# The fourth block of the recurrent gates: one plain matmul replaced by three on rounded parts, with a gather by DMA

## The chip, the cores and the metric

The kernel runs on 1 core of one Trainium2 chip. The metric is the device time of one execution in microseconds, the median of the runs shown; lower is better. TensorE is PE in the profile, VectorE DVE, ScalarE ACT, GpSimd POOL, and SP is the queue that issues most DMAs.

## The reference, cut to what matters

One inference step of two layers on 1056 tokens (1024 of a prompt, 32 of eight decoding sequences). Layer 0 is a recurrent block, layer 1 a gated linear attention. What the change touches is the pair of gates of layer 0, block diagonal with 16 blocks of 96 channels:

```python
xh = xf.reshape(Bsz, T, N_BLK, BLK_W)
r = jax.nn.sigmoid(jnp.einsum('btni,nij->btnj', xh, w_r.astype(jnp.float32)).reshape(Bsz, T, W) + b_r)
ig = jax.nn.sigmoid(jnp.einsum('btni,nij->btnj', xh, w_i.astype(jnp.float32)).reshape(Bsz, T, W) + b_i)
log_a = -LRU_C * jax.nn.softplus(-lam.astype(jnp.float32)) * r
a = jnp.exp(log_a)
bterm = jnp.sqrt(-jnp.expm1(2.0 * log_a)) * (ig * xf)
```

`xf` is the output of a causal convolution of width 4; `a` and `bterm` go into a scan over the tokens.

## The kernel before, in words

Activations stand with channels in the 128 partitions and tokens in the columns, in three chunks of 352. Products of layer 0 are exact to nearly float32 by splitting: each operand x becomes a rounded high part (an ACT copy to `F32R`) and a low part (x minus the high part, on DVE or POOL), and `mm3` (L244 to L248) makes three matmuls, high by high, high weight by low, low weight by high. A plain `F32` matmul is used in a few places, among them the one that the change replaces.

The 1536 recurrent channels are permuted into four groups of three tiles of 128. In a group, tile j holds its own block of 96 channels and, at partitions 32j to 32j+31, a third of the group's fourth block. The gates of the three own blocks are `mm3` on the tiles' parts `X` with weights `gh` and `gl` (L571), where rows and columns of the fourth block are zero. For the fourth block the three pieces of 32 partitions have to come together in one tile of 96:

- `conv` (L472): when a chunk of a tile's convolution output `t` is done, a DMA of 32 partitions puts the piece into `ST` (L512), which has all three chunks; then ACT and DVE make the parts in `X` (L514, L515).
- `lru` (L547): per chunk and per gate, a plain matmul of `ST` with the fourth block's weights `gs` (L577), a tanh into `td` (L579), and three DMAs that put its pieces back into the gate tiles `R` (L583). Two gates, three chunks, four groups: 24 such matmuls. `gs` is loaded once a group (L557).

Program order and engine order differ. Every operation is recorded in a `Flow` (L52) with an engine, an estimated length, what it reads and writes, and a priority. `Flow.run` (L188) tries several list schedules with these lengths and a random search of the opening, and emits the best in its order; so on every engine the operations of many stages are interleaved, and a changed length or dependence reorders all of layer 0. Layer 1 has a `Flow` of its own. 48 filler matmuls on constants (L739) stand at lowest priority in the opening. Products take turns in four PSUM banks `mm`, gates and norms in four banks `hg`. Weights of 128x512 go through a ring of three raw buffers `wraw` and are split into `whi` and `wlo`. In the opening, the squares of the input are summed (ACT L440 into `xo`, DVE L443) for the norm, while the first six products already run on inputs that are not yet normalized; L537 is the first evacuation of such a product by DVE.

Of the kernel before, what the change touches and what calls it, by code (L numbers as in the profile page):

```python
# [14 lines left out]
F32 = mybir.dt.float32  # L15
F32R = mybir.dt.float32r
# [22 lines left out]
NB = 8  # L39
# [175 lines left out]
def tile_trunk(ctx: ExitStack, tc: tile.TileContext, xT, prm, hc, w0, wg, wo0, w1, wo1, s_in,  # L215
# [85 lines left out]
    with ExitStack() as l0:  # L301
# [49 lines left out]
        xbs = ring("xb", 3, 384)  # L351
# [120 lines left out]
        def conv(g, head=False):  # L472

            items = []
            for j in range(3):
# [3 lines left out]
                def evac(c, ps, pk, by=None, j=j, m=m, mine=mine):  # L479
# [18 lines left out]
                    if c == 2:  # L498
                        xs = xb[:, 323:379].rearrange("p (b j) -> p b j", j=7)
                        pool(24, lambda: G.tensor_copy(xs[:, :, :3], cs[:, m]), (("hct",),), (xk,), 1)  # L500
                        act(32, lambda: S.copy(xs[:, :, 3:], ps[:, n:CH].rearrange("p (b j) -> p b j", j=4)), (pk,), (xk,), 0)
                        pool(3, lambda: G.tensor_copy(cst[:, m, 0, :], xb[:, 320:323]), (xk,), (("cst", m),), 4)
                        pool(24, lambda: G.tensor_copy(cst[:, m, 1:, :], xs[:, :, 4:7]), (xk,), (("cst", m, 1),), 4)
                        parts.append((xs, t[:, n:].rearrange("p (b j) -> p b j", j=4), lambda ap, i: ap[:, :, i:i + 4], 32))
# [6 lines left out]
                    w = slice(32 * j, 32 * j + 32)  # L511
                    dma(ST[w, chunk(c)], t[w], (tk,), (("ST", j, c),), 1, 45)  # L512
# [34 lines left out]
        def lru(g):  # L547
# [9 lines left out]
            dma(gs.rearrange("p a b -> p (a b)"), wg[g][:96, 768:], (), (("gs",),), 2, 74)  # L557
            prev = [(0.0, None)] * 3
            for c in range(NCH):
# [4 lines left out]
                tak, tik = ([("R", s, i, j) for j in range(3)] for i in range(2))  # L564
                for i, hb in ((0, hbr), (1, hbi)):
                    for j in range(3):
# [9 lines left out]

                    fl.add("PE", 0.62, lambda ps=ps, i=i, c=c: T.matmul(ps[:96, :CH], gs[:, i, :], ST[:96, chunk(c)], start=True, stop=True),  # L577
                           (("gs",), *(("ST", j, c) for j in range(3))), (pk,), 0)
                    act(CH, lambda ps=ps, i=i: S.activation(td[:, i], ps[:96, :CH], AF.Tanh, bias=hbd[:96, 4 * i + g:4 * i + g + 1],  # L579
                                                            scale=0.5), (pk, ("sm",)), (("td", i),), 2, 0.05)  # L580
                    for j in range(3):
                        w = slice(32 * j, 32 * j + 32)
                        dma(R[w, i, j], td[w, i], (("td", i),), (("R", s, i, j),), 2, 45)  # L583
# [16 lines left out]
                for j in range(3):  # L600
                    m = 3 * g + j
                    aj, bj = ab[:, j], ti[:, j]
                    if c == 2:
                        a0 = aj[:, 320:].rearrange("p (b j) -> p b j", j=4)[:, :, 0]
                        b0 = bj[:, 320:].rearrange("p (b j) -> p b j", j=4)[:, :, 0]
                        dve(8, lambda a0=a0, j=j, m=m: V.tensor_tensor(t0[:, j], a0, h0[:, m], op=ALU.mult),
                            (("a", s, j), ("hct",)), (("t0", j),), 3)
                        dve(8, lambda b0=b0, j=j: V.tensor_tensor(b0, b0, t0[:, j], op=ALU.add), (("t0", j), tik[j]), (tik[j],), 3)
                        dve(8, lambda a0=a0: V.memset(a0, 0.0), (), (("a", s, j),), 3)
# [130 lines left out]
        g0 = fixed("g0", [128, 8])  # L740
# [1197 lines left out]
```

## Time and profile before

| | |
|---|---|
| median of 3 runs | 1071.77 us (1071.49 to 1074.11) |
| the profiled execution's own time | 1068.75 us |
| its span (first to last instruction) | 1067.0 us |
| granted TensorE clock, mean | 0.993 |
| PE, DVE, ACT, POOL busy | 98%, 73%, 63%, 47% of the span |
| L577 matmuls | 24, recorded as 48 of 458 ns |

How to read it: a line is named by the number in the kernel and a group by output and inputs (`hg<-ST,gs`). A matmul's recorded length overlaps the next one's, so what a matmul costs is read from the distance between starts. An idle stretch of an engine that the end does not wait for costs nothing.

### The profile page before, as it was taken

The numbers are of one execution on the slowest core, as the hardware profiler recorded it, in microseconds if no ns is written. First come the engines' busy times: TensorE is split into PE (matmuls) and PEld (weight loads), VectorE is DVE, ScalarE is ACT, GpSimd is POOL, SyncE is SP. The second block draws the span as 40 slices with busy tenths as digits, with TensorE's granted clock in tenths as the row PEclk, the third lists the DMA queues.
The fourth block names the chain that finished last, engine by engine and source line by source line (L and its number), as shares of the span: only waits on it lengthen the run. The fifth ranks groups of instructions, "written<-read, shape, count | busy, mean of one in ns | idle before, by whom it ended". The sixth has DMA issues, their size and how long they took to land.

```text
span 1067.0 us, 25951 instructions
## 1 busy us (share of the span) xinstructions
PE 1046.7 (98%) x10120; PEld 1019.2 (96%) x10120; DVE 782.0 (73%) x1533; ACT 676.2 (63%) x1526; POOL 505.5 (47%) x528
## 2 busy tenths in 40 slices
PE   9999999999999999999989999999999989999997
PEld 9999999999999999999979999999999989999996
DVE  7999996888888688265786666656566576898636
ACT  6568656867765874243468685858586755865443
POOL 3425443454443456455544445455554454335354
PEclk9999999999999999999999999999999999999998
DMA  9111112124842685363685475756476652734634
GB/s 302 60 27 45 55 49 74 57 61 114 248 142 59 201 278 158 119 216 123 197 217 110 114 169 103 173 111 167 98 180 130 169 123 83 254 95 112 142 72 163
DMA packets 90331, 143.24 MB, mean 134 GB/s; under 512 B 11104, under 2 KB 55904, under 8 KB 90208
## 3 DMA queue, kind: packets, MB, share of 16 engines
q1 hardware_dynamic: 74656, 112.46, 33.2%
q0 software_dynamic: 13248, 26.35, 14.9%
q10 hardware_dynamic: 2304, 2.77, 0.8%
q8 instruction: 79, 1.29, 0.5%
q14 instruction: 44, 0.36, 0.1%
HBM read 81.60 MB, written 33.05 MB: 107 GB/s over the span
## 4 chain that ended last, share of the span: by engine, by line
PE 88%; DVE 7%; DMA 2%; ACT 1%; issue 1%; POOL 0%; POOLq 0%; ACTq 0%; SPq 0%; DVEq 0%
PE mm L246 24%; PE mm L248 24%; PE mm L247 24%; PE hg L1061 2%; PE hg L1278 1%; PE hg L577 1%; PE hg L1170 1%; PE hg L1280 1%; PE hg L1224 1%; PE hg L246 1%; PE hg L247 1%; PE hg L248 1%; DVE sg L1043 1%; DMA wlo<-wraw 1%; PE hg L1322 1%
## 5 line engine op out<-in xcount | busy, mean ns | idle before, releaser
L246 PE MATMUL mm<-xh,whi 128*128 128x352 f32 (+1 forms) x1147 | 354.7, 309 | 4.1 <-ACT os L1248 2.6
L247 PE MATMUL mm<-xl,whi 128*128 128x352 f32 (+1 forms) x1147 | 348.5, 304 | 0.0
L248 PE MATMUL mm<-xh,wlo 128*128 128x352 f32 (+1 forms) x1147 | 348.3, 304 | 0.0
L246 PEld LDWEIGHTS mm<-xh,whi 128*128 128x128 f32 x1147 | 215.5, 188 | 7.5 <-ACT os L1248 2.8
L247 PEld LDWEIGHTS mm<-xl,whi 128*128 128x128 f32 x1147 | 215.7, 188 | 1.7 <-issue 0.2
L248 PEld LDWEIGHTS mm<-xh,wlo 128*128 128x128 f32 x1147 | 215.6, 188 | 0.0
L333 POOL TENSOR_TENSOR wlo<-wraw,whi 128x512 fp32r<-128x512 f32 (+1 forms) x66 | 94.3, 1437 | 92.7 <-ACT whi L388 75.7
L248 PE MATMUL mm<-t,wlo 128*128 128x264 f32 x408 | 116.6, 286 | 3.8 <-DMA wlo<-wraw 3.8
L246 PE MATMUL mm<-t,whi 128*128 128x264 f32 x408 | 118.9, 291 | 0.0
L247 PE MATMUL mm<-t,whi 128*128 128x264 f32 x408 | 116.5, 286 | 0.0
L509 DVE SCALAR_TENSOR_TENSOR k<-xb,prm_sb,k 128x352 f32<-128x352 f32 (+2 forms) x144 | 90.1, 637 | 10.9 <-ACT k L506 6.1
L248 PEld LDWEIGHTS mm<-t,wlo 128*128 128x128 f32 x408 | 77.4, 190 | 4.2 <-DMA wlo<-wraw 4.2
L246 PEld LDWEIGHTS mm<-t,whi 128*128 128x128 f32 x408 | 77.6, 190 | 0.3
L247 PEld LDWEIGHTS mm<-t,whi 128*128 128x128 f32 x408 | 77.7, 190 | 0.1
L1540 DVE TENSOR_TENSOR k<-mm,k 128x264 f32<-128x264 f32 x72 | 30.6, 430 | 52.5 <-PE mm L248 50.4
L320 POOL DMA_DIRECT2D wlo<-wraw x51 | 44.5, 885 | 51.5 <-ACT wlo L319 35.6
L592 POOL TENSOR_TENSOR k<-X 128x352 f32<-128x352 f32 x36 | 43.8, 1226 | 47.6 <-DVE R L593 37.9
L246 PE MATMUL mm<-yh,whi 128*128 128x352 f32 x153 | 49.9, 326 | 0.0
L248 PE MATMUL mm<-yh,wlo 128*128 128x352 f32 x153 | 49.4, 323 | 0.0
L247 PE MATMUL mm<-yl,whi 128*128 128x352 f32 x153 | 49.4, 323 | 0.0
L388 ACT CAST whi<-wraw 128x512 fp32r<-128x512 f32 (+1 forms) x63 | 36.3, 591 | 20.2 <-DMA wraw<-in_w_dram 10.0
L320 POOL DMA_DIRECT2D wlo<-R x30 | 28.1, 936 | 43.1 <-ACT wlo L319 40.6
(425 smaller groups left out, 2724.2 us busy)
## 6 DMA issues: line engine op xcount, KB each, us to landing
wraw<-in_w_dram SPq DMA_DIRECT2D x88, 256.0 KB, 3.5
wlo<-wraw POOLq DMA_DIRECT2D x51, 256.0 KB, 4.0
wlo<-R POOLq DMA_DIRECT2D x30, 256.0 KB, 4.2
wraw<-in_wo_dram SPq DMA_DIRECT2D x37, 192.0 KB, 3.0
ysum<-sg SPq DMA_DIRECT2D x9, 528.0 KB, 4.0
si<-in_s_in_dram SPq DMA_DIRECT2D x8, 512.0 KB, 4.5
R<-in_w_dram SPq DMA_DIRECT2D x16, 256.0 KB, 3.3
out_ss_out_dram<-si SPq DMA_DIRECT2D x8, 512.0 KB, 2.7
```

The costliest lines, as they stand in the source:

```text
L246: T.matmul(out, wh, xh, start=first, stop=False, skip_group_check=chained)
L247: T.matmul(out, wh, xl, start=False, stop=False, skip_group_check=chained)
L248: T.matmul(out, wl, xh, start=False, stop=last, skip_group_check=chained)
L320: fl.add("POOL", 0.93, lambda: G.dma_start(dst.bitcast(F32), src, accum_op=ALU.add), (*r, *w), w, prio, n / 2)
L333: emit = lambda: e.tensor_tensor(b, x, a.bitcast(F32), op=ALU.subtract)
L388: act(m, lambda hi=hi, raw=raw, m=m: S.copy(hi[:, :m], raw[:, :m]), rk, (hk,), prio)
L509: dve(u, lambda src=src, dst=dst, sh=sh, k=k: V.scalar_tensor_tensor(dst, sh(src, k), pc("cw", 12 * k + m), dst, op0=ALU.mult, op1=ALU.add ...
L577: fl.add("PE", 0.62, lambda ps=ps, i=i, c=c: T.matmul(ps[:96, :CH], gs[:, i, :], ST[:96, chunk(c)], start=True, stop=True), (("gs",), *((" ...
L592: pool(CH, lambda x=x, a=a, b=b: G.tensor_tensor(x, a.bitcast(F32), b.bitcast(F32), op=ALU.add), (ak, bk), (xk,), 3)
L1043: dve(n // 2, lambda sv=sv, dv=dv, s=s, f=f: V.tensor_tensor(dv[:, :, s, :], sv[:, :, s, :], f, op=ALU.mult), (*sk, *gk), dk if i == o els ...
L1061: T.matmul(ps[32 * j:32 * j + 32, n * w:n * w + w], B[:, o:o + 32], q(slice(o, o + 32)), start=True, stop=True, tile_position=(0, 32 * j))
L1540: dve(QT, lambda: V.tensor_tensor(o[0], z[0], u[0], op=ALU.add), (z[1], u[1]), (o[1],), 0)
```

## The change

Per chunk and part, three DMAs gather the 32-partition pieces of `X` into the first chunk of `ST`, and an ACT copy takes them from there to `SH` (the copy rounds, and the parts are rounded already). The plain matmul becomes `mm3` on `SH` with split weights `sh` and `sl`, made once a group from a raw buffer by ACT and POOL. `conv` no longer fills `ST`; its other two chunks become `td`. `tails`, `g0` and `t0` move into tiles that exist.

```diff
-        td = fixed("td", [96, 2, CH])
+        SH = fixed("SH", [96, 2, CH], F32R)
-        gs = fixed("gs", [96, 2, 96])
-        t0 = fixed("t0", [128, 3, NB])
+        sh = fixed("sh", [96, 2, 96], F32R)
+        sl = fixed("sl", [96, 2, 96], F32R)
-        tails = fixed("tails", [128, 12])
+        tails = cst[:, ML - 1].rearrange("p b j -> p (b j)")[:, :12]
+        td = ST[:96, CH:].rearrange("p (a n) -> p a n", a=2)
...
-                    w = slice(32 * j, 32 * j + 32)
-                    dma(ST[w, chunk(c)], t[w], (tk,), (("ST", j, c),), 1, 45)
...
-            dma(gs.rearrange("p a b -> p (a b)"), wg[g][:96, 768:], (), (("gs",),), 2, 74)
+            raw, rk = next(raws)
+            hi, lo = (o.rearrange("p a b -> p (a b)") for o in (sh, sl))
+            dma(raw[:96, :192], wg[g][:96, 768:], (), (rk,), 2, 74)
+            act(192, lambda raw=raw: S.copy(hi, raw[:96, :192]), (rk,), (("sh",),), 2)
+            pool(192, lambda raw=raw: G.tensor_tensor(lo, raw[:96, :192], hi.bitcast(F32), op=ALU.subtract), (rk, ("sh",)), (("sl",),), 2)
...
+                xs, sk_ = [], []
+                for i in range(2):
+                    b, bk = SH[:, i], ("SH", i)
+                    for j in range(3):
+                        w = slice(32 * j, 32 * j + 32)
+                        a, ak = xpart(j, i, c)
+                        dma(ST[w, chunk(0)], a[w].bitcast(F32), (ak,), (("ST", j, 0),), 1, 45)
+                    act(CH, lambda b=b: S.copy(b, ST[:96, chunk(0)]), [("ST", j, 0) for j in range(3)], (bk,), 1)
...
-                    fl.add("PE", 0.62, lambda ps=ps, i=i, c=c: T.matmul(ps[:96, :CH], gs[:, i, :], ST[:96, chunk(c)], start=True, stop=True),
-                           (("gs",), *(("ST", j, c) for j in range(3))), (pk,), 0)
+                    fl.add("PE", 0.48, lambda ps=ps, i=i, xs=xs: mm3(ps[:96, :CH], (sh[:, i, :], sl[:, i, :]), *xs, True, True),
+                           (("sh",), ("sl",), *sk_), (pk,), 0)
```

The order of layer 0 comes out anew. On PE, the first gate of a fourth block stands like this before (`hg<-X,gh` and `gl` are the own blocks' gates, `mm<-` the input products):

```order
L247 MATMUL mm<-xl,X 128x352
L248 MATMUL mm<-xh,X 128x352
L246 MATMUL hg<-X,gh 128x352
L247 MATMUL hg<-X,gh 128x352
L248 MATMUL hg<-X,gl 128x352
L577 MATMUL hg<-ST,gs 96x352
```

and like this in the change:

```order
L246 MATMUL hg<-X,gh 128x352
L247 MATMUL hg<-X,gh 128x352
L248 MATMUL hg<-X,gl 128x352
L246 MATMUL mm<-xh,yh_151 128x352
L247 MATMUL mm<-xl,yh_151 128x352
L248 MATMUL mm<-xh,yl_154 128x352
L246 MATMUL mm<-xh,yh_151 128x352
L247 MATMUL mm<-xl,yh_151 128x352
L248 MATMUL mm<-xh,yl_154 128x352
L246 MATMUL hg<-SH,sh 96x352
L247 MATMUL hg<-SH,sh 96x352
L248 MATMUL hg<-SH,sl 96x352
```

It moved from right behind its neighbour to two input products later. Counted over PE's rows, the first gates of the first group's three chunks stand at row 331, 384 and 590 before, and at row 309, 423 and 621 in the change (four rows of fillers fewer ahead of them, and two rows more for each gate ahead).

On SP, where the first chunk is gathered, before (`ST<-k` is the convolution output, `R<-td` the pieces that go back, `wraw<-in_w` weights):

```order
L315 DMA xo_136<-in_xT_dram 128x352
L315 DMA xo_137<-in_xT_dram 128x352
L315 DMA ST<-k 32x352 x6
L315 DMA R<-td 32x352 x3
L315 DMA wraw<-in_w_dram 128x512
L315 DMA R<-td 32x352 x6
```

and in the change (`R<-ST` are now the pieces that go back):

```order
L315 DMA ST<-X 32x352 x2
L315 DMA xo_137<-in_xT_dram 128x352
L315 DMA ST<-X 32x352 x4
L315 DMA R<-ST 32x352 x3
L315 DMA ST<-X 32x352 x2
L315 DMA R<-ST 32x352 x3
L315 DMA ST<-X 32x352 x4
L315 DMA wraw<-in_w_dram 128x512 x2
```

and on ACT at the same place in the change (L494 is the evacuation that is L493 before, L508 the convolution's first term, L576 the new copy):

```order
L541 ACTIVATE sg<-mm 128x352
L576 CAST SH<-ST 96x352
L494 COPY xb_133<-mm 128x352
L508 ACTIVATE k<-xb_133,prm_sb 128x352
L576 CAST SH<-ST 96x352
L497 COPY cst<-mm 128x3
```

The gathers stand between loads and pieces that go back, and an evacuation of a product's bank stands between the two copies. In the opening PE starts before with

```order
L739 MATMUL hg<-ones 128x128 x29
L246 MATMUL mm<-xh,whi 128x352
L247 MATMUL mm<-xl,whi 128x352
L248 MATMUL mm<-xh,wlo 128x352
L246 MATMUL mm<-xh,whi 128x352
L247 MATMUL mm<-xl,whi 128x352
L248 MATMUL mm<-xh,wlo 128x352
L739 MATMUL hg<-ones 128x128 x9
```

and goes on with pieces of 2, 1, 5 and 2 fillers between products; in the change the last row is `x19`, and no filler follows. On DVE there, 12 rows of L443 on `R` stand ahead of the first L537 before, and 13 in the change.

More of the change, by code (lines that the diff above doesn't have):

```diff
@@ L350, in tile_trunk @@
         nrs = cycle([(fixed(f"nr{i}", [128, 4]), ("nr", i)) for i in range(2)])
-        xbs = ring("xb", 3, 384)
+        xbs = ring("xb", 3, 380)
         ks = [(KR[:, chunk(i)], ("k", i)) for i in range(KB)]
@@ L605, in lru @@
                         b0 = bj[:, 320:].rearrange("p (b j) -> p b j", j=4)[:, :, 0]
-                        dve(8, lambda a0=a0, j=j, m=m: V.tensor_tensor(t0[:, j], a0, h0[:, m], op=ALU.mult),
-                            (("a", s, j), ("hct",)), (("t0", j),), 3)
-                        dve(8, lambda b0=b0, j=j: V.tensor_tensor(b0, b0, t0[:, j], op=ALU.add), (("t0", j), tik[j]), (tik[j],), 3)
+                        dve(8, lambda a0=a0, m=m: V.tensor_tensor(h0[:, m], a0, h0[:, m], op=ALU.mult),
+                            (("a", s, j), ("hct",)), (("t0", m),), 3)
+                        dve(8, lambda b0=b0, m=m: V.tensor_tensor(b0, b0, h0[:, m], op=ALU.add), (("t0", m), tik[j]), (tik[j],), 3)
                         dve(8, lambda a0=a0: V.memset(a0, 0.0), (), (("a", s, j),), 3)
@@ L739, in tile_trunk @@
             fl.add("PE", 0.25, lambda: T.matmul(warm[:, :128], ones, ones, start=True, stop=True), (), (wk,), 9)
-        g0 = fixed("g0", [128, 8])
+        g0 = cst[:, ML - 1].rearrange("p b j -> p (b j)")[:, 12:20]
         dma(g0, prm[:, PRM["g0"][0]:PRM["g0"][1]], (), (("g0",),), 0, 4, S)
```

11 lines of the change are left out of this document (7 added, 4 removed).

## The prediction

> **What bounds the kernel now.** The page comes first: the span, the busy shares and the summary of the chain of work that ended last.
>
> ```profile
> span 1067.0 us, 25951 instructions
> ...
> PE 1046.7 (98%) x10120; PEld 1019.2 (96%) x10120; DVE 782.0 (73%) x1533; ACT 676.2 (63%) x1526; POOL 505.5 (47%) x528
> ...
> PE 88%; DVE 7%; DMA 2%; ACT 1%; issue 1%; POOL 0%; POOLq 0%; ACTq 0%; SPq 0%; DVEq 0%
> ```
>
> TensorE is busy for 98% and makes up 88% of the chain. A busy PE row can still hide a slow stream, so the second view cuts the span at the places that matter here: the start up to the first convolution outputs (49 us), the first group's gates (to 120), the rest of layer 0 and the first of layer 1 (to 540).
>
> ```profile
> core 0: us, PE busy (x) PEld busy (x) DVE busy (x) ACT busy (x) POOL busy (x), PEclk, DMA share, GB/s
> 0.00:49.00 49.00, 47.27 (x305) 46.18 (x306) 42.89 (x93) 30.86 (x64) 18.03 (x25) 1.00 0.59 192
> 49.00:120.00 71.00, 71.00 (x434) 69.33 (x434) 67.61 (x155) 49.61 (x100) 31.06 (x40) 1.00 0.14 39
> 120.00:540.00 420.00, 420.00 (x2783) 414.42 (x2782) 317.45 (x522) 256.61 (x498) 203.91 (x215) 1.00 0.46 138
> ```
>
> From 49 to 540 us TensorE has no idle time at all and its clock is 1.00. All 24 matmuls that the change replaces lie there, between 70 and 371 us. The third view, PE's waits over the whole span, shows where it does stand:
>
> ```profile
> PE mm L248 <- DMA wlo<-wraw: 3.8, 2, 3.5
> ...
> PE hg L739 <- DVE ones L258: 1.0, 1, 1.0
> ...
> PE mm L246 <- DVE sg L537: 0.6, 1, 0.6
> ```
>
> Of PE's waits only the last two shown are in layer 0 (at 0 and at 32 us). So in the changed stage a microsecond taken from PE's own work comes off the end of layer 0, provided that nothing new arrives late; layer 1 begins after it.
>
> **The change part by part.** *The matmul.* The timeline of PE around the first replaced matmul gives its price, since starts follow each other without a gap:
>
> ```profile
> 69.81 0.33 PE L248 MATMUL hg<-X,gl 128*128 128x352 f32 x1
> 69.97 0.76 PE L577 MATMUL hg<-ST,gs 96*96 96x352 f32 x2
> 70.30 0.59 PE L246 MATMUL hg<-X,gh 128*128 128x352 f32 x1
> 70.72 0.32 PE L247 MATMUL hg<-X,gh 128*128 128x352 f32 x1
> ```
>
> Rounded matmuls of 352 columns start 0.16 us apart (69.81 to 69.97). From the start of L577 (69.97) to that of the second matmul behind it (70.72) are 0.75 us; without the 0.16 of the one between, L577 costs 0.59. The chain of waits books the same 0.59 for it, 24 times:
>
> ```profile
> 70.13 0.59 PE hg L577 x2
> ...
> 79.53 0.59 PE hg L577 x2
> ...
> 113.42 0.59 PE hg L577 x2
> ...
> 370.35 0.59 PE hg L577 x2
> ...
> 521.75 1.03 PE hg L1061 x64
> ```
>
> In its place come three rounded matmuls of the same 352 columns. The nearest rows are those of L246 to L248 around it, which go through the same helper into the same banks: 3 x 0.16 = 0.48 us. A 96-row, 96-column rounded matmul does not occur in the trace, so I bound it: per pass at most the 0.16 of the 128-row ones, at least a quarter of L577 (0.59 / 4 = 0.148). The saving is 0.11 us (taken, same type) to 0.59 - 0.44 = 0.15 us, times 24: **2.7 us**, at most 3.6.
>
> The Trainium skill has a rule beside this: its page "TensorE: Matmul & The Clock Gate", section "Wait — 56ns, not 53.3ns?", puts back-to-back warm matmuls N / 2.4 GHz + 2.5 ns apart, which is 0.149 us for 352 columns, so that the three would take 0.45 us and the change would save 3.5 us. The trace disagrees for the rounded type: 0.16 at a granted clock of 1.00.
>
> *The gather.* 36 transfers of a convolution output (k to ST) go; 72 of its rounded parts (X to ST) come, and 24 ACT copies from ST to SH. Rows for both:
>
> ```profile
> L315 SPq DMA_DIRECT2D ST<-k x36: 507/512/1391, 49.3 to 356.5; - x36
> ...
> DMA to landing us min/median/max: 1.8/1.8/5.1
> ```
>
> ```profile
> L514 ACT CAST X<-k 128x352 fp32r<-128x352 f32 x36 | 17.5, 486 | 25.3 <-DVE k L509 25.2
> L579 ACT ACTIVATE td<-hg,smalls 96x352 f32<-96x352 f32 x24 | 13.2, 550 | 5.0 <-PE hg L577 4.8
> ```
>
> SP issues 36 more, 36 x 0.51 = 18 us between 49 and 371. ACT gets 24 x 0.49 = 11.7 us: six in 49 to 120 us, where it is busy 49.6 of 71, eighteen behind that, where it is busy 256.6 of 420. That cover holds: cost nothing. What the edit lengthens is the way from a finished part to the matmul: before one issue and landing, 1.8 us. Now the low half reuses ST and waits for the copy of the high half, so with both halves ready at once it is three issues and a landing (2 x 0.51 + 1.8 = 2.8), a copy (0.5), 2.8 and 0.5 again: 6.6 us. What hides it is the order. DVE's timeline gives the end of the last part of each chunk of the first group, the tightest:
>
> ```profile
> 54.17 0.52 DVE L515 TENSOR_TENSOR X<-k,X 128x352 fp32r<-128x352 f32 x1
> ...
> 74.74 0.52 DVE L515 TENSOR_TENSOR X<-k,X 128x352 fp32r<-128x352 f32 x1
> ...
> 109.31 0.95 DVE L515 TENSOR_TENSOR X<-k,X 128x352 fp32r<-128x352 f32 x2
> ```
>
> Ends at 54.7, 75.3 and 110.3, plus 6.6: 61.3, 81.9 and 116.9. The matmuls of these chunks stood at 70.1, 79.5 and 113.4 (the chain's L577 rows). In the new PE order they stand 18 rows ahead, 39 behind and 27 behind the old place (rows that the change adds, and merged filler rows, set off), at 0.16 us a row: 67.2, 85.7 and 117.7. Margins 5.9, 3.8 and 0.8 us, so I take 0; the ends are 0 and, with the worst landing, the price of the third rival.
>
> New waits have queues behind them. On SP a gather of the low half waits for ACT, and behind it stand the loads of the next weights and the R rows that the gates of the other block need; on ACT the copy to SH waits for the DMA, and behind it stands the evacuation xb<-mm of a product bank. Both are visible in the order rows. The nearest existing case is ACT waiting in L579 for PE (5.0 us in 24 times, row above), and no PE idle came of it. The group's small weights go through a raw buffer, an ACT cast and a POOL subtraction instead of straight into gs, four times: at most 0.5 on ACT each (192 columns against the 352 of the row above), and on POOL a subtraction whose price I need not know: POOL stands 256 of the 491 us (two window rows). It also takes one place of three in the ring of raw buffers; nothing.
>
> Storage: td in ST's other chunks, tails and g0 in the last convolution state, t0 into h0. They add waits only where the last group's state is written, when tails and g0 are long done: nothing.
>
> *The opening.* All ops are ordered afresh, so the first 49 us change too. The 48 filler matmuls are the same number; before they stand in six pieces, now in two. The timeline of PE behind one of these pieces:
>
> ```profile
> 13.19 0.41 PE L246 MATMUL mm<-xh,whi 128*128 128x352 f32 x1
> 13.44 0.32 PE L247 MATMUL mm<-xl,whi 128*128 128x352 f32 x1
> ```
>
> A product behind a filler starts its second matmul 0.25 us after its first (13.19, 13.44) instead of 0.16; three fewer such places give 0.3. PE's wait of 0.6 for L537 is DVE emptying the first bank. In the new order DVE does 13 instead of 12 sums of squares ahead of that:
>
> ```profile
> L443 DVE TENSOR_TENSOR R<-R,xo 128x352 f32<-128x352 f32 x14 | 8.2, 585 | 0.6
> ```
>
> That may make the wait 0.6 longer; the other rows ahead of it are nearly the same set, and DVE is busy 42.9 of 49 us. I take 0, bounds -0.9 (wait and switches gone) and +2.0 (three or four such sums late).
>
> **Sum.** The profiled execution took 1068.75 us: span 1067.0 and 1.75 around it. 24 x (0.59 - 0.48) = 2.7 off gives a span of 1064.3 and a time of 1066.05. The median shown, 1071.77, is 3.0 above that execution; the same saving there gives **1069.1 us**, 0.25% less.
>
> **Rivals.**
>
> *A pass costs 0.148.* If the three matmuls run like passes of L577, or the opening loses its 0.9 us of wait and switches, the saving is 3.6: 1068.2. Against the first speaks every rounded 352-column row; for the second, that in the new order DVE makes the xl parts ahead of the sums, so that nothing stands before 22 us.
>
> *The saving is absorbed.* PE waits 3.5 us for wlo<-wraw at 545 us. If that transfer were held by something that does not move with layer 0's end, the wait would grow by 2.7: 1071.8. Against it: its loads read xn, which the last products of layer 0 write, and the order of layer 1 is the same on every engine.
>
> *The gather comes late (slower).* Place: the chunks of the first group, 60 to 120 us, where DVE is busy 67.6 of 71 us, so that parts are made just ahead of use. Price: landings of 5.1 instead of 1.8 in both halves make the way 6.6 longer; less the margins of 5.9, 3.8 and 0.8 that is 0.7, 2.8 and 5.8, so 9.3 - 2.7 = 6.6 slower, 1078.4. It decides from 2.7 us of standing in all, and from 5.9 it is 0.3% slower. For it speak the 5.1 and the weight loads on the same queue. Against it stands the median, 1.8. [...]
>
> *It doesn't do what it says.* Rounded matmuls on these operands could run as four passes each: 3 x 0.59 = 1.77, 24 x 1.18 = 28 us slower, 1100. The rows of L246 to L248, same helper and types, exclude it nearly.
>
> **How the numbers follow.** A measurement of this kernel can tell about 0.3%, 3.2 us, from no change; the forecast lies just inside. Forecast with up to 1.5 us either way: 0.57. The 0.148 pass or the better opening: 0.18. Absorbed, or the opening 2 us worse: 0.13. Late gather: 0.11. Four passes: 0.01. Faster by over 0.3% (below 1068.55): all of the second and a third of the first, 0.37. Slower by over 0.3%: 0.10 of the late gather and the four passes. The rest, 0.53, is within. Range: from 1066.5 (3.6 and 0.9 together, and 0.8 for the spread of runs) to 1073.5 (opening 2.0 worse and a few short stands), leaving out most of the late gather.
>
> **What would show it.** PE's group hg<-SH,sh should have 24 per line and no L577; starts 0.16 apart; the PE window up to the same work's end without idle; the start of layer 1's first L1061 near 519.0 instead of 521.75; ACT busy about 12 us more; PE's waits in layer 1 as before. It is wrong if PE waits for ACT SH, for DMA wraw in 60 to 400 us, or if the wait at 545 grows by what was saved.

## The result and the profile after

| | before | after |
|---|---|---|
| median, runs side by side on one chip | 1071.63 us (4 runs, 1070.85 to 1074.11) | 1077.34 us (4 runs, 1076.25 to 1077.48) |
| ratio | | 1.0063, 95% interval 1.0043 to 1.0083 |
| the profiled execution | 1068.75 us, span 1067.0 | 1077.32 us, span 1075.5 |

The change made the kernel 0.6% slower: 5.7 us between the medians of four runs each, 6.7 us by the ratio, where 2.7 us less were forecast. The two profiled executions lie 8.5 us apart, since that of before is 3 us below its median. Lines of `conv`, `lru` and what follows moved down by up to 13: L577 is now the triple L246 to L248 on `SH`, L579 is L592, L592 is L605, L669 is L682, L1061 is L1074.

The page of after, the same lines as shown of before:

```profile
span 1075.5 us, 26055 instructions
...
PE 1050.4 (98%) x10144; PEld 1027.5 (96%) x10144; DVE 775.4 (72%) x1533; ACT 683.3 (64%) x1554; POOL 506.1 (47%) x532
...
PE 80%; DVE 9%; DMA 3%; ACT 3%; issue 2%; POOL 2%; SPq 0%; ACTq 0%; POOLq 0%; DVEq 0%
```

PE is as busy as before by the page, but its part of the chain fell from 88% to 80%: other work now ends last in places. The stretches say where (columns: stretch, length, then busy time of PE, PEld, DVE, ACT and POOL, PE's clock, DMA share, GB/s):

```profile
0.00:49.00 49.00, 45.64 (x284) 44.84 (x285) 41.56 (x86) 29.59 (x62) 19.70 (x27) 0.97 0.60 192
49.00:120.00 71.00, 71.00 (x443) 70.77 (x442) 62.96 (x157) 51.05 (x105) 25.55 (x37) 1.00 0.17 45
120.00:340.00 220.00, 220.00 (x1373) 219.99 (x1372) 178.70 (x289) 155.51 (x310) 98.91 (x110) 1.00 0.34 100
340.00:460.00 120.00, 115.79 (x711) 113.65 (x711) 87.66 (x149) 73.48 (x145) 64.54 (x68) 1.00 0.62 187
```

From 49 to 340 us PE has no idle time, the first group's gates among it. It stands in two places: in the opening (45.64 of 49 us, 47.27 before, and at a clock of 0.97) and from 340 to 460 us, the last group (115.79 of 120, 120 before). PE's waits up to 540 us name them:

```profile
PE mm L246 <- DVE sg L537: 2.3, 1, 2.3
PE mm L248 <- POOL wlo L682: 1.3, 2, 0.7
PE mm L248 <- POOL wlo L333: 1.3, 1, 1.3
PE mm L246 <- DVE k L657: 1.1, 1, 1.1
PE hg L752 <- DVE ones L258: 1.0, 1, 1.0
PE mm L246 <- ACT xb L502: 0.4, 1, 0.4
```

The first is the opening's (0.6 before). The other new ones, 4.1 us in five stands, all lie between 352 and 443 us. None is a wait for the fourth block's inputs: PE waits for low parts of weights (`wlo`, POOL) and for banks that DVE and ACT empty late.

The product matmuls of layer 0 come in the same sequence in every kernel here, so their starts can be laid side by side. Counted from 0, the 600th stands at 127.9 us before, behind the opening and the first group; the 2400th at 453.3, behind the last group. In after they stand 2.5 and 8.5 us later, and so does all of layer 1 (7.8 us at the 3000th, 8.6 at the 6000th): it is shifted, nothing more is lost in it.

### The profile page after: what moved, and what is told of

Same layout as the page of the kernel before. It is cut to its first block, busy times and chain, and to the rows that moved or that the text cites. A ratio compares the mean times of both kernels' runs of the same rounds, so it can differ in the third digit from the quotient of the medians.

```text
span 1075.5 us, 26055 instructions
## 1 busy us (share of the span) xinstructions
PE 1050.4 (98%) x10144; PEld 1027.5 (96%) x10144; DVE 775.4 (72%) x1533; ACT 683.3 (64%) x1554; POOL 506.1 (47%) x532
## 4 chain that ended last, share of the span: by engine, by line
PE 80%; DVE 9%; DMA 3%; ACT 3%; issue 2%; POOL 2%; SPq 0%; ACTq 0%; POOLq 0%; DVEq 0%
PE mm L246 22%; PE mm L248 22%; PE mm L247 21%; PE hg L1074 2%; PE hg L1183 1%; DVE k L511 1%; PE hg L1291 1%; PE hg L1237 1%; PE hg L1293 1%; PE hg L246 1%; PE hg L248 1%; PE hg L247 1%; DVE R L444 1%; DMA R<-ST 1%; PE hg L1335 1%
## 5 line engine op out<-in xcount | busy, mean ns | idle before, releaser
L246 PE MATMUL mm<-xh,whi 128*128 128x352 f32 (+1 forms) x1147 | 351.9, 307 | 2.6 <-ACT os L1261 1.3
L248 PE MATMUL mm<-xh,wlo 128*128 128x352 f32 (+1 forms) x1147 | 349.5, 305 | 2.0 <-POOL wlo L333 1.3
L246 PEld LDWEIGHTS mm<-xh,whi 128*128 128x128 f32 x1147 | 215.6, 188 | 4.5 <-ACT os L1261 1.5
L248 PEld LDWEIGHTS mm<-xh,wlo 128*128 128x128 f32 x1147 | 215.9, 188 | 2.5 <-POOL wlo L333 1.6
L333 POOL TENSOR_TENSOR wlo<-wraw,whi 128x512 fp32r<-128x512 f32 (+1 forms) x66 | 93.0, 1423 | 77.8 <-ACT whi L389 64.9
L248 PE MATMUL mm<-t,wlo 128*128 128x264 f32 x408 | 116.6, 286 | 3.3 <-DMA wlo<-wraw 3.3
L246 PE MATMUL mm<-t,whi 128*128 128x264 f32 x408 | 118.9, 291 | 0.0
L511 DVE SCALAR_TENSOR_TENSOR k<-xb,prm_sb,k 128x352 f32<-128x352 f32 (+2 forms) x144 | 84.3, 595 | 9.5 <-ACT k L508 6.1
L248 PEld LDWEIGHTS mm<-t,wlo 128*128 128x128 f32 x408 | 77.3, 189 | 3.5 <-DMA wlo<-wraw 3.5
L246 PEld LDWEIGHTS mm<-t,whi 128*128 128x128 f32 x408 | 77.6, 190 | 0.5 <-ACT k L1530 0.2
L605 POOL TENSOR_TENSOR k<-X 128x352 f32<-128x352 f32 x36 | 42.9, 1199 | 61.3 <-DVE R L606 48.3
L246 PE MATMUL mm<-yh,whi 128*128 128x352 f32 x153 | 49.7, 325 | 1.5 <-DVE k L657 1.1
L248 PE MATMUL mm<-yh,wlo 128*128 128x352 f32 x153 | 49.5, 324 | 0.6 <-POOL wlo L682 0.6
L587 ACT ACTIVATE R<-hg,smalls 128x352 f32<-128x352 f32 x72 | 37.7, 549 | 15.0 <-DVE R L626 7.3
```

Source lines behind the costliest of these rows:

```text
L246: T.matmul(out, wh, xh, start=first, stop=False, skip_group_check=chained)
L248: T.matmul(out, wl, xh, start=False, stop=last, skip_group_check=chained)
L333: emit = lambda: e.tensor_tensor(b, x, a.bitcast(F32), op=ALU.subtract)
L511: dve(u, lambda src=src, dst=dst, sh=sh, k=k: V.scalar_tensor_tensor(dst, sh(src, k), pc("cw", 12 * k + m), dst, op0=ALU.mult, op1=ALU.add ...
L587: act(CH, lambda ps=ps, R=R, i=i, j=j, hb=hb, m=m: S.activation(R[:, i, j], ps[:, :CH], AF.Tanh, bias=hb[:, m:m + 1], scale=0.5), (pk, ("s ...
L605: pool(CH, lambda x=x, a=a, b=b: G.tensor_tensor(x, a.bitcast(F32), b.bitcast(F32), op=ALU.add), (ak, bk), (xk,), 3)
```

## The experiments

Theories at the start. **Way of the gather**: parts reach the triple over three transfers and a copy, twice in a row (high half, then low half), through one pair of buffers; what depends on them comes late. **Order**: any new order of layer 0 costs, since the one before happens to fit the chip. All results, ratios against runs of before on the same chip; the last two columns are the shift in us of the 600th and 2400th product against the profiled execution of before (an execution's start alone moves by up to 1 us):

| kernel | ratio | 95% interval | 600th | 2400th |
|---|---|---|---|---|
| after | 1.0063 | 1.0043 to 1.0083 | +2.5 | +8.5 |
| after_search | 1.0050 | 1.0031 to 1.0069 | +2.5 | +8.3 |
| before_nosearch | 1.0016 | 0.9996 to 1.0036 | +0.9 | +2.1 |
| before_est | 1.0028 | 1.0005 to 1.0050 | +0.7 | +2.6 |
| direct | 1.0066 | 1.0046 to 1.0087 | +1.5 | +8.6 |
| mm_alone | 0.9967 | 0.9957 to 0.9978 | -0.6 | -2.5 |
| no_gather | 1.0020 | 1.0004 to 1.0035 | +3.1 | +2.7 |
| pin_open | 1.0050 | 1.0032 to 1.0069 | +1.5 | +6.2 |
| parts | 1.0029 | 1.0015 to 1.0042 | 0.0 | +1.9 |
| one_sum (same order as after) | 1.0062 | 1.0048 to 1.0076 | +1.3 | +8.3 |
| gather_unread | 1.0045 | 1.0032 to 1.0059 | +0.1 | +2.3 |
| parts_pin | 1.0033 | 1.0021 to 1.0044 | +0.7 | +1.1 |
| open_strict | 1.0035 | 1.0017 to 1.0053 | -1.7 | +5.1 |
| no_gather_order | 0.9977 | 0.9961 to 0.9992 | -1.0 | -2.2 |
| parts_order | 1.0021 | 1.0002 to 1.0040 | -1.0 | +1.2 |
| after_order | 1.0083 | 1.0061 to 1.0104 | -1.2 | +7.2 |
| parts_pool | 1.0011 | 0.9994 to 1.0027 | -1.0 | +1.3 |

**The planner's search and its estimate.** In after the random search of the opening found only plans that tie with the one it began with, and a tie keeps the old one. So: after with the search's plan, before without a search, and before with nothing but the estimate changed.

```diff
-        return min(best, self.plan(key), key=lambda g: g[0])
+        return min(self.plan(key), best, key=lambda g: g[0])
```

> The change, with one edit: where the searched order plans the same end as the unsearched one, the searched one is kept, so that the opening is searched as it was before. Theory (half the loss is the opening, half the serial gather in the last group): PE's stand on L537 near 32 us falls from 2.3 to about 0.6 and the clock stays up, so 2 to 3 us less than the change, about 1074.7. Rival 1 (all of the loss is the gather): 1077, the stand on L537 may go but the end does not move. Rival 2 (the orders are chance): anything between 1069 and 1080, with stands at places that the change did not have.

```diff
-            fl.run(SEARCH, 60.0)
+            fl.run(0, 60.0)
```

> The kernel before, with the search of the opening left out. If the opening's order by itself is worth 2.4 us: 1073 to 1074.5, with PE standing about 2 us on L537 near 32 us and no stand from 60 to 540 us. If the search is worth nothing on the chip: 1071.6.

```diff
-                    fl.add("PE", 0.62, lambda ps=ps, i=i, c=c: T.matmul(ps[:96, :CH], gs[:, i, :], ST[:96, chunk(c)], start=True, stop=True),
+                    fl.add("PE", 0.48, lambda ps=ps, i=i, c=c: T.matmul(ps[:96, :CH], gs[:, i, :], ST[:96, chunk(c)], start=True, stop=True),
```

> The kernel before, with only the planner's length of the fourth block's matmul changed from 0.62 to 0.48: the same work in another order. If orders are equal as long as the planner sees no idle PE: 1071.6 within 1. If another order alone costs microseconds, as rival 2 says: 2 us or more away from it, with PE stands in layer 0 that before did not have.

1.0050, 1.0016 and 1.0028. The searched plan does not get the loss back, and losing the search costs before at most 0.4%. The third computes exactly what before does, with the same instructions, and is 0.3% slower by the order alone.

**direct.** The parts go by DMA straight into `SH`; no `ST`, no copies.

```diff
-                        dma(ST[w, chunk(0)], a[w].bitcast(F32), (ak,), (("ST", j, 0),), 1, 45)
-                    act(CH, lambda b=b: S.copy(b, ST[:96, chunk(0)]), [("ST", j, 0) for j in range(3)], (bk,), 1)
+                        dma(b[w].bitcast(F32), a[w].bitcast(F32), (ak,), ((*bk, j),), 1, 45)
+                        sk_.append((*bk, j))
                     xs.append(b)
-                    sk_.append(bk)
```

> The change, but the gather writes straight into SH: no pass through ST, no copy on ACT, the two parts' gathers do not wait for each other. The order comes out anew (with a searched opening). Theory (the long way over ST makes the last group late, and POOL behind it): no PE stands at 350 to 440 us, and all of 2.7 us of PE work saved is seen: 1069 to 1070. Rival (72 transfers and their issues on SP are the trouble, not ST and the copy): stands at 350 to 440 us remain, 1073 to 1076.

1.0066, as slow. The copies are gone and the halves no longer wait for each other, but `SH` still holds one chunk's pair, and now PE stands for the gather itself. PE's waits of direct from 340 to 460 us:

```profile
PE hg L247 <- DMA SH<-X: 2.0, 2, 1.4
PE hg L246 <- ACT R L586: 0.9, 1, 0.9
PE hg L246 <- DMA SH<-X: 0.8, 1, 0.8
PE hg L247 <- DVE X L515: 0.4, 1, 0.4
```

So "over `ST`" is not the whole of the way's price; both share the single pair of buffers and SP's queue (and direct has an order of its own, which is not set apart here).

**mm_alone.** Before, its order untouched, with the triple on parts that are there anyway.

```diff
-                    fl.add("PE", 0.62, lambda ps=ps, i=i, c=c: T.matmul(ps[:96, :CH], gs[:, i, :], ST[:96, chunk(c)], start=True, stop=True),
-                           (("gs",), *(("ST", j, c) for j in range(3))), (pk,), 0)
+                    (a, ak), (b, bk) = xpart(0, 0, c), xpart(0, 1, c)
+                    fl.add("PE", 0.62, lambda ps=ps, i=i, a=a, b=b: mm3(ps[:96, :CH], (gh[:96, i, :96], gl[:96, i, :96]), a[:96], b[:96], True, True),
+                           (ak, bk, ("gh", 0), ("gl", 0), ("gs",), *(("ST", j, c) for j in range(3))), (pk,), 0)
```

> The kernel before, its order of instructions kept, with the three rounded matmuls in the place of each plain one; their operands are the parts of block 0, so the fourth block's own inputs are left out of the computation (they are still gathered by the 36 old transfers). Only the price of the matmul changes. If the saving is real and reaches the end: 24 x 0.11 = 2.7 us less, ratio 0.9975, TensorE without idle from 49 to 540 us, layer 1 starting 2.7 us sooner. Rival: something behind TensorE takes the saving (a load or a vector engine that does not move along): ratio 1.000 and new stands of TensorE.

0.9967: 3.5 us less (2.4 to 4.6). The saving is real and reaches the end. With 340 to 460 us as full as before:

```profile
340.00:460.00 120.00, 120.00 (x750) 119.79 (x750) 76.49 (x130) 65.84 (x127) 59.99 (x61) 1.00 0.57 178
```

**no_gather and parts.** After without gather and copies (the triple reads the neighbour's parts), and after with the old gather of `t` into `ST` and the split made from there. The heart of the edit for parts:

```diff
...
+                xs, sk_ = [SH[:, 0], SH[:, 1]], [("SH", 0), ("SH", 1)]
+                stk = [("ST", j, c) for j in range(3)]
+                act(CH, lambda c=c: S.copy(SH[:, 0], ST[:96, chunk(c)]), stk, (("SH", 0),), 1)
+                dve(CH, lambda c=c: V.tensor_tensor(SH[:, 1], ST[:96, chunk(c)], SH[:, 0].bitcast(F32), op=ALU.subtract),
+                    (*stk, ("SH", 0)), (("SH", 1),), 1, True)
...
```

> The changed kernel without its 72 gathering transfers and 24 copies; the triples read the parts of block 0, so the fourth block's own inputs are left out. The order is planned anew. Theory 'serial way of the gather': the stands of TensorE between 340 and 450 us (5.6 us in the changed kernel) are gone, what may stay is the opening (2.4 us); ratio 0.9975 to 1.000. Rival 'any new order costs': ratio 1.003 to 1.006 again, with stands in the same stretch.

> The changed kernel with the old gather: 36 transfers of the convolution outputs into all three pieces of ST, as before, and there 12 ACT copies (high) and 12 DVE subtractions (low) in place of 72 transfers and 24 copies; the gate outputs wait in the pieces of ST that are used up. It computes everything. The way from the convolution output to the triple is 1.8 + 0.5 + 0.5 = 2.8 us, and between one chunk's last triple and the next chunk's first only the copy and the subtraction, 1.0 us, in place of two gathers and two copies (over 6 us). Theory 'serial way': stands of TensorE in 340 to 450 us below 1 us, ratio 0.998 to 1.001. Rival 'any new order costs': ratio 1.003 to 1.006.

Both took away the stands of 340 to 460 us (PE 120.00 of 120 in no_gather), so those belong to the gather from the parts. But no_gather is still at 1.0020, 5.7 us above mm_alone (1.0020 less 0.9967, times 1070), with nothing gathered; 3.7 of them are there at the 600th product. Neither theory alone holds.

**pin_open, one_sum, open_strict: the opening.** In after DVE empties the first bank (L537) late. DVE's timeline of after, and POOL's beside it:

```profile
31.31 1.16 DVE L444 TENSOR_TENSOR R<-R,xo 128x352 f32<-128x352 f32 x2
...
32.57 1.60 DVE L444 TENSOR_TENSOR R<-R,xo 128x352 f32<-128x352 f32 x1
34.09 0.51 DVE L537 TENSOR_TENSOR sg<-mm,R 128x352 f32<-128x352 f32 x1
```

```profile
32.52 1.27 POOL L333 TENSOR_TENSOR yl<-wraw,yh 128x512 fp32r<-128x512 f32 x1
```

The last sum ahead of L537 is the 13th (before had 12 there). It starts 0.05 us behind a POOL operation and takes 1.60 us, where the two ahead of it take 1.16 together; L537 starts at 34.09 (31.49 before). The same is seen at two other of the 13 sums that start while POOL makes a `yl` part (1.65 us at 22.62, 1.42 at 29.15); the other ten take 0.52 or 0.53.

```diff
...
-            best = self.search(best, tries, first)
+            best = self.plan([OPENING.get(i, k) for i, k in enumerate(best[1])])
```

> The changed kernel, whole, with the operations that stood in the first 45 us of the kernel before planned at their old places (a table of 330 start times takes the place of the search). If the 2.4 us lost in the opening are the new order of the opening and nothing else: TensorE's stands up to 49 us as before (about 2.4 us less than in the changed kernel), the stands of 340 to 450 us stay, ratio 1.003 to 1.004. Rival: the opening's loss has another cause, ratio 1.005 to 1.006 as in the changed kernel.

```diff
-            best = self.search(best, tries, first)
+            best = self.plan([t + 4.0 * (i == 328) for i, t in enumerate(best[1])])
```

> The changed kernel, whole, with one of DVE's sums of squares (the 13th, 1.60 us in the changed kernel's trace, against 0.52 where POOL is idle) placed behind the first emptying of a bank (L537) in place of ahead of it. Theory 'one sum too many ahead of L537': TensorE's stand at 32 us shrinks from 2.5 to about 1 us, the slow stretch behind it (starts 0.29 apart) goes, together 2 to 3 us: ratio 1.002 to 1.004, the stands of 340 to 450 us stay. Rival 'DVE is behind as a whole there': the stand moves to the next wait for DVE and the ratio stays at 1.005 to 1.006.

```diff
...
+        for a, b in CHAIN if tries else ():
+            self.ops[b][3].add(a)
         self.after = [[] for _ in self.ops]
...
-            best = self.search(best, tries, first)
+            best = self.plan(ORDER)
```

> The changed kernel, whole, with DVE and TensorE held to the order of the kernel before for the first 45 us (a chain of waits in the planner, a table of start times), so that no 13th sum stands ahead of the first emptying of a bank. Theory 'the opening's loss is DVE's order': TensorE's stand at 32 us falls from 2.5 to about 1 us and the slow stretch behind it goes, 2 to 3 us in all; the stands between 340 and 450 us (5.6 us) stay; ratio 1.003 to 1.004. Rival 'the opening is not it': ratio 1.005 to 1.006.

The first two missed their aim. The planner never lets an engine idle in its model, so a later due time did not hold the sum back: pin_open still had a sum (1.62 us) ahead of L537 and stood 1.8 us; one_sum came out in the order of after on all engines, and is a repeat of it (1.0062). With a dependence in place of a due time, open_strict has the order wanted. DVE's timeline of open_strict (L594 is the sum, L687 is L537):

```profile
29.65 1.14 DVE L594 TENSOR_TENSOR R<-R,xo 128x352 f32<-128x352 f32 x2
...
30.79 1.38 DVE L687 TENSOR_TENSOR sg<-mm,R 128x352 f32<-128x352 f32 x3
```

PE's wait there is 0.5 us, the 600th product is 1.7 us ahead of before, and the ratio falls from 1.0063 to 1.0035: the opening's order is worth some 3 us. The two intervals overlap, so the size is loose; one_sum, a repeat of after, is at 1.0062, and the 600th product of open_strict comes 4.2 us ahead of that of after and 3.0 ahead of that of one_sum. The stands of the last group are all still there.

**no_gather_order, after_order: before's order without and with the gather.** Both keep DVE and PE to before's order for 45 us and take before's start times for the rest, by the same edit as open_strict with tables of their own.

> The kernel without the gather (the triples read block 0's parts, so the fourth block's own inputs are left out) once more, but in the order of the kernel before: DVE and TensorE held to it for 45 us, the rest taken from its start times. Theory 'the new order was the price of 5.7 us between the kernel with the matmul alone and the one without the gather': ratio 0.996 to 0.998. Rival 'the other edits are' (the new storage, the small weights through a raw buffer, an ACT cast and a POOL subtraction): ratio 1.000 to 1.003.

> The changed kernel, whole and with its gather, in the order of the kernel before as far as its operations are in both (DVE and TensorE held to it for 45 us, the rest from its start times; where the gather doesn't let it, operations come later: the last group's fourth-block gates are planned at 349 to 383 us, those of the kernel without the gather in the same order at 343 to 364). Beside that kernel (ratio 0.9977) it has only the 72 transfers and 24 copies and the wait for them, so the difference is the price of the gather. Theory 'the gather has a price of its own': ratio 1.001 to 1.005, with stands of TensorE of 3 to 6 us between 200 and 450 us. Rival 'only the order costs': ratio 0.997 to 0.999.

0.9977 and 1.0083. The first is mm_alone again (intervals overlap): storage and small weights cost nothing that shows, and the 4.6 us to no_gather (1.0020) are order. Between the two lies the gather, and with it whatever of that order it does not allow (see the planned times above): 1.06%, 11.3 us (8.5 to 14.2 with both intervals; 9.4 at the 2400th product), more than either expectation had. Up to 540 us PE's only wait without it is 1.0 us at the start. With it, the four largest are (L807 is L657, L726 the copy to `SH`):

```profile
PE mm L396 <- DVE k L807: 4.4, 5, 2.1
PE hg L397 <- ACT SH L726: 1.4, 1, 1.4
PE hg L902 <- DVE ones L408: 1.0, 1, 1.0
PE mm L396 <- DVE xo L807: 0.9, 1, 0.9
```

Half of these stands lie between 219 and 305 us, ahead of the last group, and most are for product banks that DVE empties late, none for weights from POOL. So the gather costs in this order too, but not at the same places as in after.

How the gather stretches the work is seen at the fourth block's tanh, six of them in the last group (first and last start at the end of the row): before, no_gather_order, after_order and after.

```profile
L579 ACT ACTIVATE td<-hg,smalls x6: 551/552/553, 349.0 to 374.9; 96x352 f32<-96x352 f32 x6
```

```profile
L728 ACT ACTIVATE ST<-hg,smalls x6: 550/552/554, 347.4 to 372.8; 96x352 f32<-96x352 f32 x6
```

```profile
L742 ACT ACTIVATE ST<-hg,smalls x6: 542/550/553, 356.5 to 394.0; 96x352 f32<-96x352 f32 x6
```

```profile
L592 ACT ACTIVATE ST<-hg,smalls x6: 539/549/553, 359.5 to 401.3; 96x352 f32<-96x352 f32 x6
```

25 to 26 us from first to last become 38 and 42. The timeline of after shows the cycle, first the end of PE's second triple of a chunk and the start of the next chunk's first, then ACT's copies to `SH` (L576):

```profile
363.14 0.32 PE L248 MATMUL hg<-SH,sl 96*96 96x352 f32 x1
...
375.27 0.32 PE L246 MATMUL hg<-SH,sh 96*96 96x352 f32 x1
```

```profile
363.50 0.49 ACT L576 CAST SH<-ST 96x352 fp32r<-96x352 f32 x1
...
373.09 0.49 ACT L576 CAST SH<-ST 96x352 fp32r<-96x352 f32 x1 [1.24 <-DMA ST<-X]
...
380.10 0.49 ACT L576 CAST SH<-ST 96x352 fp32r<-96x352 f32 x1
...
392.17 0.49 ACT L576 CAST SH<-ST 96x352 fp32r<-96x352 f32 x1 [1.12 <-DMA ST<-X]
```

The triple ends reading `SH` at 363.46, and 0.04 us later the next chunk's high part is copied into it; its low part, through the same `ST`, follows 9.6 us after, and in the next chunk 12.1 us after. The gather itself stands in SP's queue (start, duration of the issue):

```profile
364.04 1.78 SPq L315 DMA_DIRECT2D R<-ST  x3
365.92 0.53 SPq L315 DMA_DIRECT2D wraw<-in_w_dram  x1
...
367.97 0.42 SPq L315 DMA_DIRECT2D x1b<-xb  x1
368.81 2.17 SPq L315 DMA_DIRECT2D ST<-X  x3
```

`ST` is free from 364.0, but SP first issues gate rows, weights and the output's loads and stores, with hardly a pause, and reaches the gather at 368.81. What comes behind the gates is late in turn. POOL's timeline of after:

```profile
374.13 0.94 POOL L605 TENSOR_TENSOR k<-X 128x352 f32<-128x352 f32 x1 [13.40 <-DVE R L606]
...
391.00 0.94 POOL L605 TENSOR_TENSOR k<-X 128x352 f32<-128x352 f32 x1 [6.98 <-DVE R L606]
392.40 3.08 POOL L605 TENSOR_TENSOR k<-X 128x352 f32<-128x352 f32 x2 [0.46 <-DVE R L606]
395.44 5.39 POOL L333 TENSOR_TENSOR wlo<-wraw,whi 128x512 fp32r<-128x512 f32 x3
```

And the waits of all engines from 340 to 400 us:

```profile
POOL k L605 <- DVE R L606: 21.3, 4, 13.4
...
DVE R L606 <- DMA R<-ST: 7.8, 2, 4.0
```

POOL stands 13.4 us and then 7.0 us before L605, since its buffer is free only when DVE's L606 has used it, and L606 waits for the gate rows that come back (`R<-ST`); before, the longest such wait was 5.59, ahead of 358.11. Behind the second wait in POOL's queue stand the low parts of the next weights, which come at 395.44 in a row, and PE waits for them at 396 (L333). It also waits for low parts at 439 and 442 (L682); POOL itself waited for a load of weights in between (5.3 us, up to 411.94), so that these two stands still come from the late gates is not shown.

**gather_unread.** All transfers and copies, but the triple doesn't read them.

```diff
-                    fl.add("PE", 0.48, lambda ps=ps, i=i, xs=xs: mm3(ps[:96, :CH], (sh[:, i, :], sl[:, i, :]), *xs, True, True),
-                           (("sh",), ("sl",), *sk_), (pk,), 0)
+                    us, uk_ = [xpart(0, v, c)[0][:96] for v in range(2)], [xpart(j, v, c)[1] for j in range(3) for v in range(2)]
+                    fl.add("PE", 0.48, lambda ps=ps, i=i, us=us: mm3(ps[:96, :CH], (sh[:, i, :], sl[:, i, :]), *us, True, True),
+                           (("sh",), ("sl",), *uk_), (pk,), 0)
```

> The changed kernel with all its transfers and copies, but the triples read the parts of block 0 and not SH, so nothing waits for the gather (the fourth block's own inputs are left out of the computation). It separates the load of the 72 transfers and 24 copies from the wait for them. Theory 'serial way' (the wait is the price): TensorE's stands of 340 to 450 us are below 1 us as in the kernel without the gather, the last gates of the last group end before 385 us; ratio 1.000 to 1.003 (the opening's loss stays). Rival 'load' (SP, ACT and POOL have too much to do): stands of 4 to 6 us in that stretch again, ratio 1.005.

1.0045, between no_gather (1.0020) and after (1.0063), with stands of 1.6 us from 340 to 460 where after has 4.2 (PE busy 118.43 and 115.79 of 120) and the last tanh at 380.8 in place of 401.3. Neither expectation held as it stood. By the stands the wait makes most, 2.6 us of 4.2, and the load of 72 transfers and 24 copies the rest; by the ratios the load is 2.7 us (0.5 to 4.9) and the wait 1.9 (-0.6 to 4.5). Each kernel also has its own order, so the two are not told apart.

**parts_pin, parts_order, parts_pool: is there a faster whole version?** The split made on the chip from the old `ST`, in before's order, wished for, then held in the opening, then with the subtraction on POOL (the edit shown is this last step).

```diff
-                dve(CH, lambda c=c: V.tensor_tensor(SH[:, 1], ST[:96, chunk(c)], SH[:, 0].bitcast(F32), op=ALU.subtract),
-                    (*stk, ("SH", 0)), (("SH", 1),), 1, True)
+                pool(CH, lambda c=c: G.tensor_tensor(SH[:, 1], ST[:96, chunk(c)], SH[:, 0].bitcast(F32), op=ALU.subtract),
+                     (*stk, ("SH", 0)), (("SH", 1),), 1)
```

> The kernel with the old gather (36 transfers of the convolution outputs, then 12 ACT copies and 12 DVE subtractions on the chip) and the rounded triples, whole, in an order taken from the kernel before as far as its operations are in both (a table of start times; the planner's model has TensorE without idle and the last group's fourth-block gates at 343 to 367 us, where the kernel before has 345 to 367). If the matmul's saving is real and only the way of the gather and the new order took it: stands up to 540 us as before, ratio 0.997 to 0.999, the first whole version that is faster than both. Rival: the added 24 operations or any new order cost what was saved, ratio 1.000 to 1.003.

> The whole computation with the old gather (36 transfers, then 12 ACT copies and 12 DVE subtractions) and the rounded triples, DVE and TensorE held to the order of the kernel before for 45 us and the rest taken from its start times. Before, with the order of the first 45 us only wished for, two normalising operations of 2.1 us came ahead of the emptying of a bank, TensorE stood 1.9 us there and the ratio was 1.0033. If opening and last group are both as before: ratio 0.997 to 0.999, faster than both kernels. Rival 'the 24 added operations cost the rest': ratio 1.000 to 1.003.

> As the whole version with the old gather in the old order (ratio 1.0021; TensorE stood 3.3 us behind DVE between 271 and 286 us and 1.7 us at 31 us), but its 12 subtractions are made by POOL and not by DVE. Theory 'DVE is the engine that is full': the stands at 271 to 286 us go, ratio 0.998 to 1.000. Rival 'POOL then delays the low parts of the weights': new stands for wlo, ratio 1.002 or more.

1.0033, 1.0021 and 1.0011: better than after, not faster than before. The gates of the last group are back (351.0 to 378.1 in parts_order) and nothing stands behind 340 us, but PE now stands at 271 to 286 us behind DVE, which empties the output products late (waits of parts_order, L803):

```profile
PE mm L394 <- DVE xo L803: 1.6, 2, 0.8
PE mm L394 <- DVE sg L686: 1.5, 1, 1.5
PE hg L898 <- DVE ones L406: 1.0, 1, 1.0
PE mm L394 <- DVE k L803: 1.0, 2, 0.7
```

Moved to POOL, the subtraction leaves short stands near the same place (1.6 us for `xo` and `k`); the split costs about what the matmul saves, or a little more. A second pair of buffers for the gather was not tried. That the single pair sets the cycle is read from the timeline above and not shown by a run of its own.

## Why the prediction was wrong, step by step

1. *The matmul*: right. The triples start 0.16 us apart (399.49, 399.66, 399.82 in after), 24 per line, and mm_alone gives 3.5 us (2.4 to 4.6; 2.5 at the 2400th product) where 2.7 were forecast and 3.6 was the bound. The rows speak for 0.16 and not for the 0.149 of the quoted rule, with which the prediction's sum comes to 3.4 us and not the 3.5 written there.
2. *The gather*: "cost nothing" is the step that failed. The first group's margins held: no stand from 49 to 340 us. But I looked at the way from a finished part to its matmul, and only in the group that I called the tightest. I left out that it is also a cycle, because one pair of buffers serves all chunks: from a chunk's last triple to the next chunk's first there are a copy, three transfers and a copy. And I priced a half of it, with its copy, at 3.3 us (2.8 and 0.5) as if SP were free; in the last group, where SP issues the output's loads and stores, it took 9.6 and 12.1. The last tanh of the gates starts at 401.3 in place of 374.9. Price in before's order: 11.3 us; in the order that the planner made around it, some 4.6 us (1.0063 less 1.0020, times 1070; 1.9 to 7.3 with both intervals). That the gather costs is shown by runs; that it costs by this cycle is read from the timeline.
3. *New waits on SP and ACT*: up to 540 us PE has no wait for `SH` or for `wraw` in after; the engine that I set aside was POOL. I counted its idle time (256 of 491 us) as cover. (The case that I leaned on, ACT waiting for PE in L579, was 4.8 us in 8 waits, not 5.0 in 24.) In after its queue was what mattered: it stood 13.4 us and 7.0 us behind late gates, and the weights were behind it.
4. *Storage and small weights*: right (no_gather_order, 0.9977, against mm_alone, 0.9967).
5. *The opening*: the cause was named (a 13th sum ahead of L537) and its price taken as 0, with 2.0 as the end. It is some 3 us by open_strict. The sum took 1.60 and not the 0.585 of the row quoted: it started beside a POOL operation, and the quoted mean mixes sums of 0.52 with one of 1.43 that did so too (at 28.02 in before). In this execution the stand was also followed by a stretch at half pace (below). The bound for the fillers was a little off: from six pieces to two are four fewer places, 0.36 us, and not three.
6. *The sum*: -2.7 became, by ratios times 1070 us, -2.5 (no_gather_order), +4.6 for a new order without the gather (no_gather; its 600th product is already 3.1 us late, so most of it is the opening), +4.6 for the gather: 6.7 us, which is the ratio of 1.0063; the medians of those eight runs are 5.7 apart. Outside the opening the prediction had no term for a new order. How the 9.2 us divide depends on the order in which they are compared: in before's order the gather alone brings 11.3.

Of the rivals, "the saving is absorbed" did not happen (PE's wait for `wlo<-wraw` is 3.3 us in after, 3.8 before). "The gather comes late" had the right kind of cause; its 1078.4 lies near the 1077.3 measured by luck: it put the price in the first group, from slow landings, and there nothing was lost. Its landing of 5.1 us was misread, too: that is the load of weights into `ST` at 10.3 us, and the longest landing of a gather before is 3.6, with which the rival's sum gives 0.1 us slower in place of 6.6. It had 0.11 because I judged the order by margins in the group where parts are made just ahead of use, and not where the most work hangs on the gates.

## What to carry to other kernels

When a transfer comes between a producer and a matmul, work out two times: from ready to use, and from one use of its buffer to the next; compare the second with the spacing of the uses in the tightest stretch of the order. Off the critical path, ask of each engine not how busy it is but what stands behind a late operation in its queue. In a kernel whose order is searched, a new length or dependence rearranges everything: here that alone was worth some 3 to 5 us, more than the saving, so measure the edit once in the old order before judging it.

## What the runs showed of the hardware

A stand of PE is sometimes followed by matmuls at half pace. PE's timeline of after and of one_sum, whose instructions have the same order, at the same place:

```profile
34.66 0.66 PE L246 MATMUL mm<-xh,yh 128*128 128x352 f32 x1 [2.31 <-DVE sg L537]
35.12 0.49 PE L247 MATMUL mm<-xl,yh 128*128 128x352 f32 x1
35.41 0.49 PE L248 MATMUL mm<-xh,yl 128*128 128x352 f32 x1
```

```profile
34.94 0.43 PE L246 MATMUL mm<-xh,yh 128*128 128x352 f32 x1 [2.33 <-DVE sg L537]
35.20 0.32 PE L247 MATMUL mm<-xl,yh 128*128 128x352 f32 x1
35.36 0.32 PE L248 MATMUL mm<-xh,yl 128*128 128x352 f32 x1
```

Stands of 2.31 and 2.33 us; in the first, starts are 0.29 us apart for some 3 us, which costs 1.4 us more. The granted clock shows it: over 32 to 49 us its mean (third number from the end) is 0.90 in after, as much as half the clock for 3.4 of the 17 us, and 1.00 in one_sum and before.

```profile
32.00:49.00 17.00, 14.69 (x81) 14.19 (x80) 16.39 (x31) 8.76 (x20) 8.34 (x10) 0.90 0.27 73
```

Of the stands over 0.9 us in layer 0, such a stretch followed one of 1.2 us (after_search), 1.4 (direct), 1.8 (pin_open), 1.9 (open_strict), 2.3 (after) and 3.0 (no_gather) and, among others, did not follow those of 2.0 (gather_unread), 2.1 (after_order) and 2.3 (one_sum). So the length of a stand does not decide it alone, and the price of one varies from run to run. The Trainium skill, "TensorE: Matmul & The Clock Gate", section "What's actually happening", has the slow state come after at least one idle window of about 3.4 us; here it came after less than half of that.
